# Three edits to a hybrid trunk layer on one core: margins for GpSimd, finer parts of the output projection, and another order of the front's loads and splits

## The chip, the cores and the metric

The kernel runs on 1 core of one Trainium2 chip. The metric is the device time of one execution in microseconds (us), lower is better; a kernel's time is the median of its runs. Engines: PE is TensorE (matmul), PEld its weight loads, DVE is VectorE, ACT ScalarE, POOL GpSimd, SP SyncE, which here issues nearly all DMAs.

## The reference

One decoder layer on x of 256 positions by 2048 features, float32. A norm, one input projection for all mixers, three mixers, an output projection with residual, a second norm and a gated MLP with a causal convolution, and a final norm:

```python
def reference(x, ...):
    h = rmsnorm(x, norm1_w)
    x = x + token_mixer(h, w_in, ..., w_out)
    h = rmsnorm(x, norm2_w)
    x = x + conv_ffn(h, ffn_w_up, ffn_conv_w, ffn_conv_b, ffn_w_down)
    return rmsnorm(x, final_norm_w)

def token_mixer(h, w_in, ...):
    proj = h @ w_in                      # D_IN = 6924 columns
    r_q, r_k, r_v, r_g, m_qk, m_v, m_o, m_gates, s_u = jnp.split(proj, splits, axis=-1)
    ret_out = silu(r_g) * head_groupnorm(retention(rotary(r_q), rotary(r_k), r_v), ret_gn_w)
    m_qk = silu(causal_dwconv(m_qk, mlstm_conv_w, mlstm_conv_b))
    i_pre, f_pre = jnp.split(m_gates + mlstm_gate_b, 2, axis=-1)
    mlstm_out = sigmoid(m_o) * head_groupnorm(mlstm(mq, mk, m_v, i_pre, f_pre), mlstm_gn_w)
    s5_out = s5(s_u, ...)                # diagonal complex state space model, gelu, gated by g @ glu_w
    return jnp.concatenate([ret_out, mlstm_out, s5_out], axis=-1) @ w_out
```

Retention and mLSTM have 6 heads of 128 features each, S5 has 512 features; together the 2048 rows of `w_out`. The MLP is 2048 to 2 x 5632 to 2048.

## The kernel before, in words

**Matmuls.** Every float32 weight chunk `wr` (up to 128 x 1024, from DRAM into one of four buffers) is split into a high part `wh` (a cast on ACT, `highs_to`) and a low part `wl` (a subtraction on DVE, `lows_to`); activations are split in the same way, the high part `d[:, :256]` by ACT, the low part `d[:, 256:]` by DVE. In the feature-major tiles (`fm_tile`, `fm_part`) the weights are stationary: for each K tile of 128 rows one matmul of 512 columns (high weights with both parts of x) and one of 256 (low weights with the high part of x). An output tile f is 128 features by 256 positions in one PSUM bank; 16 K tiles come as two chunks of 8. `chunk(i)` issues loads five items ahead, casts three and subtractions two ahead.

**Order.** Up to the end of the output projection the order of instructions on each engine is made by a planner in the kernel's own code: clocks `clk.pe`, `clk.dve`, `clk.act`, `clk.pool` are moved on by estimated costs (`run`), and everything beside the main chain of matmuls is a generator that yields what it waits for: `("dve", t)` until the DVE clock reaches t, `("pe", t)` until PE's does, `("obj", f)` until a condition holds. `pump()` runs between blocks of matmuls and steps the tasks that are due, first `hi_tasks` (evacuations of PSUM), then `lo_tasks` (heads, gates, S5) as long as the DVE clock is at most 0.35 us ahead of PE's. The clocks place instructions; on the chip the engines wait for each other by semaphores only. `after(t)` is such a wait for a result of POOL.

**Front.** x comes as 16 K tiles of 128 features. The first projection, `u` for S5, has four output tiles and is run K tile by K tile as the data arrive: `kts` holds four steps j of one K tile (weights 128 x 512) and then six of two (128 x 1024). Step j waits for its data, casts the weights, splits x by `n1` (from the parameters `pp0`), subtracts the weights, and issues 8 matmuls per K tile. `fill(n)` puts n of the 29 small DVE steps of the S5 exponentials (`s5_exps`, 128 x 16 each) in between; their 14th result starts POOL's chain `s5_params`. `square` collects x squared for the norm from step 4 on. SP issues x and weights in turn; ACT's queue issues `pp0`. Nine matmuls on ones (`warm`) precede the first real one. After the loop come six tiles for retention's q and k; between their blocks `first_norm` sums the squares on PE, POOL takes the power −1/2 (`rsqrt_`), and two transposes on PE (`norm_row`) make the row scale `rbc`.

**Heads.** `head_norm` normalises six heads (statistics on DVE, the power on POOL, scaling on ACT), multiplies by the gate, then for each head: two transposes on PE, the high part on ACT, the low part on DVE, into `mix[base + h]`. `mix[0..5]` is retention, `mix[6..11]` mLSTM, `mix[12..15]` S5 after `glu`. The gate of the second half of the mLSTM heads is the last tile (`tm_tile(7, ...)`) before the output projection.

**Output projection.** `parts` is its order: ((f, ...), k0, k1) takes K tiles k0 to k1 of tiles f; `None` stands for the S5 gate `glu`. PSUM has four `acc` banks and one `pair` of two. Tiles below `EARLY` = 4 are evacuated after K tile 12 (`early_evac`, which adds x) and get a second bank for K tiles 12 to 16. Tiles from `LATE` = 10 on are run whole after all parts. `out_evac` adds x or the early sum, splits by `n2` for the MLP and adds the square. Before a part the planner's loop `while any(k not in mix ...)` pumps until all its inputs are in the order.

After that the compiler's own scheduling takes over (MLP and final norm), which the change does not touch.

Of the kernel before, what the change touches and what calls it, by code (L numbers as in the profile page):

```python
# [40 lines left out]
def kernel(ctx: ExitStack, tc: tile.TileContext, a: dict, out: bass.AP):  # L41
# [54 lines left out]

    def after(t):

        return "dve", max(x[3] for x in wrote[t.tensor.name]) + 0.1

    def finish(gen):

# [223 lines left out]
    def add_stream(ap, n, step=CH):  # L326
        first = len(items)
        for c in range(0, n, step):
# [14 lines left out]
    st_tm.append(add_stream(a["wtm"][6], KT * 384, 768))  # L343


    EARLY, LATE = 4, 10

    parts = [((f,), 0, 8) for f in range(4)] + [((0, 1), 8, 12), ((2, 3), 8, 12)]
    parts += [((f,), 0, 8) for f in range(4, 8)] + [((4, 5), 8, 12), ((6, 7), 8, 12), ((8,), 0, 8), None,
                                                    ((9,), 0, 8), ((8, 9), 8, 12)]  # L350
    parts += [((f, f + 1), 12, 16) for f in (4, 6, 8, 0, 2)]
    wo_first = {}
    for part in parts:
        if part is None:
            st_glu = add_stream(a["glu"], 4 * 512)
        else:
            fs, k0, k1 = part
            wo_first[part] = len(items)
            items.append(([a["wout"][f][:, k0 * 128:k1 * 128] for f in fs], CH))
    st_out = [None] * LATE + [add_stream(a["wout"][f], KT * 128) for f in range(LATE, 16)]  # L360
    st_up = [add_stream(a["wup"][f], KT * 128) for f in range(2 * NFF)]
    st_dn = [add_stream(a["wdn"][f], NFF * 128) for f in range(14)]
    st_last = add_stream(a["wdt"], NFF * 256)
# [13 lines left out]
    def loads_to(i):  # L377
        while nxt[0] <= min(i, len(items) - 1):
            j = nxt[0]
            ap, n = items[j]  # L380
            if NS <= j < NU:

                t = s4()
            else:
                t = reuse("wr", wraw.tile([128, CH], F32, tag="wr", name=f"wr{j}"), 4)
            for i, z in enumerate(ap):
                nc.sync.dma_start(out=t[:, i * n // len(ap):(i + 1) * n // len(ap)], in_=z)
            if not auto[0]:
                free_at = max([x[3] for x in was_read.get(t.tensor.name, ())], default=0.0)
                clk.dma = max(clk.dma, free_at + 1.3) + n / 703.0  # L390
                landed(t, clk.dma + 0.91)
            if later:

                dst, src = later.pop(0)
                nc.sync.dma_start(out=dst, in_=src)
                clk.dma += free(dst) / 703.0
                landed(dst, clk.dma + 0.91)
                loaded.add(dst.tensor.name)
            raw[j] = t
            nxt[0] += 1  # L400
# [612 lines left out]
    def gates():  # L1013
# [19 lines left out]
            G.scalar_tensor_tensor(p, p, 1.0 / k, z2, op0=ADD, op1=MUL)  # L1033
        G.scalar_tensor_tensor(p, p, 1.0, z, op0=ADD, op1=MUL)
        G.scalar_tensor_tensor(lf, p, -2.0, lf, op0=MUL, op1=ADD)
        yield "dve", wrote[lf.tensor.name][-1][3]
        yield "pe", clk.dve + 0.2
        yield from grab("mis")
        ps = mis_t()
# [122 lines left out]
    manual = ctx.enter_context(ExitStack())  # L1162
    manual.enter_context(tc.manual_schedule())

    nc.scalar.dma_start(out=pp0, in_=a["pp"][:, :NP0])
    nc.gpsimd.memset(onesm, 1.0)

# [5 lines left out]
    warm = mis_t()  # L1173
    for _ in range(9):
        mm(warm[:, :128], lhsT=onesm, rhs=onesm, start=True, stop=True)
    clk.pe = 4.8

    xr, xat = [None] * 8, {}

# [15 lines left out]
    add(ret_heads())  # L1195
    add(gates())
    add(ml_heads())
    clk.dve = clk.pool = 3.3
    add(s5_params(s5_den()))
    add(s5_inputs())  # L1200
    for c in range(4):
# [10 lines left out]
    def first_norm():  # L1212
        r, ps = yield from norm_root(1)
        yield after(r)
        yield have(ident, rot)
        yield "pe", max(x[3] for x in wrote[r.tensor.name]) + 0.3
        bc = yield from norm_row(1, r, ps)
        rh = tn([128, 2])
        V.tensor_scalar(rh, r, 0.5, None, op0=MUL)
        for i in range(2):  # L1220
            V.tensor_tensor(rot[:, i * T:(i + 1) * T], rot[:, i * T:(i + 1) * T], bc, op=MUL)
        st.update(r=r, rh=rh, rbc=bc, cosr=rot[:, :T], sinr=rot[:, T:])
# [20 lines left out]
            next(exps, None)  # L1243

    for j, ks in enumerate(kts):
        fill(3 if j < 2 else 6)
        pump(until=max(last(raw[j].tensor.name), xat[ks[-1]]))
        if j > 1:
            highs_to(j)
        for k in ks:  # L1250
            d = s2(F32R)
            S.activation(d[:, :T], xr[k // 2][:, (k % 2) * T:(k % 2 + 1) * T], AF.Copy, scale=P("n1", k))
            xs.append(d)
        if j > 1:
            lows_to(j)
        for k in ks:
            V.scalar_tensor_tensor(xs[k][:, T:], xr[k // 2][:, (k % 2) * T:(k % 2 + 1) * T], P("n1", k),
                                   xs[k][:, :T], op0=MUL, op1=SUB)
        fill(4 if j < 2 else 0)
        lows_to(j)  # L1260
        loads_to(j + 4)
        if j + 4 == NU:
            rot = s2()
            raws = [s2() for _ in range(4)]
            later += [(ident, a["ident"]), (rot, a["rot"])]
            later += [(raws[i], a["s5b" if i < 2 else "s5c"][i % 2]) for i in range(4)]
            later += [(pp1, a["pp"][:, NP0:])]
            st["raws"] = raws
        if j >= NU - 6 and len(sqs) < 8:
            square()  # L1270
        hl = split.pop(j)
        for i, k in enumerate(ks):
            o = [slice(i * 512 + f * 128, i * 512 + (f + 1) * 128) for f in range(4)]
            for f in range(4):
                mm(ups[f], lhsT=hl[0][:, o[f]], rhs=xs[k], start=(k == 0), stop=False)
            for f in range(4):
                mm(ups[f][:, T:], lhsT=hl[1][:, o[f]], rhs=xs[k][:, :T], start=False, stop=(k == KT - 1))
# [105 lines left out]
    for part in parts:  # L1383
        if part is None:
            for f in range(EARLY, LATE, 2):
                get_x(f)
            glu()
            continue
        fs, k0, k1 = part
        if k0 == 8 and fs[0] < EARLY:  # L1390
            get_x(fs[0])
        while any(k not in mix for k in range(k0, k1)):
            clk.pe += 0.25
            pump()
        again = k0 == 12 and fs[0] < EARLY
        for f in fs:
            if f == 8 and k0 == 0:
                while len(bu) < 4:
                    clk.pe += 0.25
                    pump()  # L1400
                need("pair")
                room["pair"] -= 1
                pair = reuse("pair", ps_m.tile([128, 1024], F32, tag="pair", name=name("wo")), 1)
                wps[8], wps[9] = pair[:, :512], pair[:, 512:]
            elif f < 8 and (k0 == 0 or again):
                wps[f] = acc_t()
        hl = chunk(wo_first[part])
        for i, f in enumerate(fs):
            fm_part(wps[f], [z[:, i * CH // 2:] for z in hl], range(k0, k1), k0, mix,
                    12 if f < EARLY and not again else KT, first=12 if again else 0)  # L1410
        for f in fs:
            if f < EARLY and k1 == 12:
                add(early_evac(f, wps[f]), hi=True)
            elif k1 == KT:
                add(out_evac(f, wps[f], "acc" if f < 8 else "half"), hi=True)
        pump()
    get_x(LATE)
    for f in range(LATE, 16):
        if f + 2 < 16:
            get_x(f + 2)  # L1420
        add(out_evac(f, fm_tile(st_out[f], mix)), hi=True)
        pump()
    drain()
    xs2 = [xs2[f] for f in range(16)]
# [223 lines left out]
```

## Time and profile before

| | us |
|---|---|
| median of 3 runs (lowest, highest) | 1150.41 (1149.25, 1152.27) |
| time of the profiled execution | 1148.91 |
| its span, first to last instruction | 1147.1 |
| PE busy / DVE busy / ACT busy / POOL busy | 1131.2 / 879.0 / 628.0 / 76.5 |
| front: first real matmul to the end of `u` | 4.84 to 30.96 |
| output projection, first block | 299.45 |
| first tile that is run whole (f10) | 367.55 |

Rows of the timeline read: start us, duration us, engine, line, operation, out<-in, partitions x elements, count of merged instructions, and in brackets the idle time before it and who ended it. A line is often that of a helper (L235 every matmul, L183 every DVE operation, L218 every POOL operation), so rows are told apart by tiles and shapes: `wh`, `wl` are weights, `mis<-ident,s` a transpose of a head, `mis<-ident,t` a transpose of small rows such as the norm's. Rows of the waits read: engine and line that waited, for whom, total us, times, longest.

### The profile page before, as it was taken

The page shows a single profiled execution, that of the slowest core. Times are in us where ns is not written, and L with a number is a line of the kernel's source. Part 1 is how long each engine was busy: PE and PEld are TensorE (multiplying, and loading weights), DVE is VectorE, ACT ScalarE, POOL GpSimd, SP SyncE. Part 2 cuts the span into 40 slices and gives each one's busy share as a digit, 9 for nine tenths or more (in the row PEclk, how much of TensorE's full clock was granted, in tenths as well). Part 3 has the DMA queues.
Part 4 walks back from the last instruction along what each step waited for, and adds up shares of the span by engine and source line. Part 5 has one row for each costly group of instructions (what it writes and reads, how often), then busy time and mean ns, then how long its engine had stood idle before and what let it go on. Part 6 is the DMA issues. An engine that isn't in the chain of part 4 may idle for free.

```text
span 1147.1 us, 18124 instructions
## 1 busy us (share of the span) xinstructions
PE 1131.2 (99%) x6672; PEld 1010.3 (88%) x6672; DVE 879.0 (77%) x1527; ACT 628.0 (55%) x988; POOL 76.5 (7%) x171
## 2 busy tenths in 40 slices
PE   8999999999999999999999999999999999999997
PEld 7899889999888888888888888888888888888897
DVE  8899999999979777777777777777777655444454
ACT  7665565455647655555555555555555444444442
POOL 8407040010000000000000000000000000000000
PEclk9999999999999999999999999999999999999999
DMA  8657545556665655555555555555556566666662
GB/s 316 201 159 241 178 141 161 147 151 172 210 205 191 200 181 193 191 189 195 184 185 190 194 191 188 192 184 186 191 192 197 177 193 178 193 188 193 189 192 106
DMA packets 67625, 215.21 MB, mean 188 GB/s; under 512 B 7632, under 2 KB 9936, under 8 KB 67536
## 3 DMA queue, kind: packets, MB, share of 16 engines
q1 hardware_dynamic: 67392, 214.01, 58.8%
q8 instruction: 52, 0.85, 0.3%
q14 instruction: 37, 0.30, 0.1%
q10 hardware_dynamic: 144, 0.04, 0.0%
HBM read 211.92 MB, written 2.10 MB: 187 GB/s over the span
## 4 chain that ended last, share of the span: by engine, by line
PE 94%; POOL 3%; DVE 2%; issue 0%; DMA 0%; DVEq 0%; POOLq 0%
PE acc L235 90%; PE mis L235 3%; POOL t L218 2%; DVE s L183 2%; PE wo L235 1%; POOL tp L218 1%; DVE wl L183 1%; PE mis L239 0%; DMA pp<-in_pp_dram 0%; DVEq L1644 0%; PE pj L235 0%; DVE t L183 0%; DVEq L183 0%; POOLq L218 0%
## 5 line engine op out<-in xcount | busy, mean ns | idle before, releaser
L193 ACT CAST wh<-wr 128x1024 fp32r<-128x1024 f32 (+3 forms) x409 | 407.7, 998 | 417.2 <-PE acc L235 256.5
L235 PE MATMUL acc<-s,wh 128*128 128x512 f32 x2372 | 578.0, 392 | 6.0 <-DVE s L183 5.8
L183 DVE TENSOR_TENSOR wl<-wr,wh 128x1024 fp32r<-128x1024 f32 (+3 forms) x409 | 462.6, 1155 | 147.2 <-PE acc L235 96.1
L235 PEld LDWEIGHTS acc<-s,wh 128*128 128x128 f32 x2372 | 433.3, 188 | 90.0 <-DVE s L183 8.1
L235 PEld LDWEIGHTS acc<-s,wl 128*128 128x128 f32 x2372 | 309.8, 191 | 15.6 <-issue 0.7
L235 PE MATMUL acc<-s,wl 128*128 128x256 f32 x2372 | 317.1, 283 | 0.0
L183 DVE TENSOR_TENSOR s<-s,s 128x256 f32<-128x256 f32 (+5 forms) x264 | 124.7, 487 | 47.6 <-ACT s L202 41.5
L235 PE MATMUL acc<-wh,s 128*128 128x384 f32 (+2 forms) x632 | 158.0, 329 | 0.0
L183 DVE SCALAR_TENSOR_TENSOR s<-s,pp,s 128x255 f32<-128x255 f32 (+3 forms) x244 | 116.3, 479 | 6.1 <-ACT s L202 2.9
L235 PEld LDWEIGHTS acc<-wh,s 128*128 128x128 f32 x632 | 112.1, 189 | 2.0 <-ACT wh L193 1.1
L235 PE MATMUL acc<-wl,s 128*128 128x384 f32 (+2 forms) x316 | 103.0, 326 | 0.0
L183 DVE TENSOR_TENSOR s<-acc,s 128x256 f32<-128x256 f32 x142 | 59.2, 420 | 45.0 <-ACT s L193 41.7
L202 ACT ACTIVATE s<-s,pp 128x256 f32<-128x256 f32 (+1 forms) x146 | 82.2, 567 | 13.7 <-DVE s L183 12.6
L202 ACT ACTIVATE s<-s 128x256 f32<-128x256 f32 (+2 forms) x105 | 44.8, 428 | 34.6 <-DVE s L183 34.4
L218 POOL TENSOR_TENSOR t<-t,neg_half 128x2 f32<-128x2 f32 (+1 forms) x4 | 2.5, 633 | 882.3 <-DVE t L183 882.3
L235 PEld LDWEIGHTS acc<-wl,s 128*128 128x128 f32 x316 | 59.6, 189 | 0.1
L193 ACT COPY s<-acc 128x256 f32<-128x256 f32 x140 | 50.0, 360 | 11.1 <-PE acc L235 11.1
L235 PE MATMUL acc<-g,wh 128*128 128x512 f32 x196 | 49.5, 392 | 0.0
L183 DVE TENSOR_TENSOR s<-s,rbc 128x256 f32<-128x256 f32 x106 | 44.6, 424 | 5.6 <-ACT rbc L193 2.5
L235 PEld LDWEIGHTS acc<-g,wh 128*128 128x128 f32 x196 | 35.8, 188 | 6.9
L235 PEld LDWEIGHTS acc<-g,wl 128*128 128x128 f32 x196 | 25.4, 191 | 1.1
L235 PE MATMUL mis<-s,s 128*32 128x256 f32 (+6 forms) x216 | 25.8, 343 | 0.0
(107 smaller groups left out, 466.2 us busy)
## 6 DMA issues: line engine op xcount, KB each, us to landing
wr<-in_wup_dram SPq DMA_DIRECT2D x176, 512.0 KB, 4.5
wr<-in_wdn_dram SPq DMA_DIRECT2D x70, 512.0 KB, 4.2
wr<-in_wtm_dram SPq DMA_DIRECT2D x56, 384.0 KB, 3.3
wr<-in_wfm_dram SPq DMA_DIRECT2D x36, 512.0 KB, 4.1
wr<-in_wout_dram SPq DMA_DIRECT2D x22, 512.0 KB, 4.6
wr<-in_wdt_dram SPq DMA_DIRECT2D x11, 512.0 KB, 3.7
wr<-in_wout_dram SPq DMA_DIRECT2D x20, 256.0 KB, 3.8
s<-in_x_dram SPq DMA_DIRECT2D x14, 256.0 KB, 5.6
```

Source lines behind the costliest of these rows:

```text
L183: return real(o, *args, **kw)
L193: return nc.scalar.copy(o, i)
L202: return nc.scalar.activation(o, i, fn, **kw)
L218: return real(o, *args, **kw)
L235: nc.tensor.matmul(o, lhsT=lhsT, rhs=rhs, start=start, stop=stop)
```

## The change

1. Margins: `after` waits for POOL's result plus 1.0 us (0.1 before); the gates' transposes wait 3.0 us longer, the norm's transposes 1.8 (0.3 before).
2. Output projection: `EARLY` is 6 and `LATE` 12. Tiles 0 to 3 run K tiles 0 to 6 first, all four, then 6 to 12; tiles 4 to 11 in parts of 8 and 4 as before, with 10 and 11 in the `pair`. The last K tiles 12 to 16 run in pairs of tiles, and the whole tiles 12 to 15 (an integer in `parts`) stand between these pairs. x for tiles 12 and 14 is loaded just ahead of them.
3. Front: the first weight tile is issued on ACT's queue, ahead of `pp0`; each step splits x before it casts and subtracts the weights; the high part of K tile 0 is made on DVE; the small steps are spread, four per step in steps 0 to 3 and fewer per K tile later.

The planner's starting values (`clk.pe`, `clk.dve`, `clk.pool`) change with it.

```diff
     def after(t):
-        return "dve", max(x[3] for x in wrote[t.tensor.name]) + 0.1
+        return "dve", max(x[3] for x in wrote[t.tensor.name]) + 1.0
...
-    EARLY, LATE = 4, 10
-    parts = [((f,), 0, 8) for f in range(4)] + [((0, 1), 8, 12), ((2, 3), 8, 12)]
-    parts += [((f,), 0, 8) for f in range(4, 8)] + [((4, 5), 8, 12), ((6, 7), 8, 12), ((8,), 0, 8), None,
-                                                    ((9,), 0, 8), ((8, 9), 8, 12)]
-    parts += [((f, f + 1), 12, 16) for f in (4, 6, 8, 0, 2)]
+    EARLY, LATE = 6, 12
+    parts = [((f,), k, k + 6) for k in (0, 6) for f in range(4)]
+    parts += [((4,), 0, 8), ((5,), 0, 8), ((4, 5), 8, 12)] + [((f,), 0, 8) for f in range(6, 10)]
+    parts += [((6, 7), 8, 12), ((10,), 0, 8), None, ((8, 9), 8, 12), ((11,), 0, 8), ((10, 11), 8, 12)]
+    parts += [((6, 7), 12, 16), ((8, 9), 12, 16), 12, ((10, 11), 12, 16), ((0, 1), 12, 16), 13, ((2, 3), 12, 16), 14,
+              ((4, 5), 12, 16), 15]
...
+        elif isinstance(part, int):
+            st_out[part] = add_stream(a["wout"][part], KT * 128)
         else:
             fs, k0, k1 = part
             wo_first[part] = len(items)
-            items.append(([a["wout"][f][:, k0 * 128:k1 * 128] for f in fs], CH))
+            items.append(([a["wout"][f][:, k0 * 128:k1 * 128] for f in fs], len(fs) * (k1 - k0) * 128))
...
-                nc.sync.dma_start(out=t[:, i * n // len(ap):(i + 1) * n // len(ap)], in_=z)
+                (nc.sync if j else nc.scalar).dma_start(out=t[:, i * n // len(ap):(i + 1) * n // len(ap)], in_=z)
...
-        yield "dve", wrote[lf.tensor.name][-1][3]
+        yield "dve", wrote[lf.tensor.name][-1][3] + 3.0
...
+    loads_to(0)
     nc.scalar.dma_start(out=pp0, in_=a["pp"][:, :NP0])
...
-    clk.pe = 4.8
+    clk.pe = 4.5
...
-    clk.dve = clk.pool = 3.3
+    clk.dve = clk.pool = 3.7
...
-        yield "pe", max(x[3] for x in wrote[r.tensor.name]) + 0.3
+        yield "pe", max(x[3] for x in wrote[r.tensor.name]) + 1.8
...
     for j, ks in enumerate(kts):
-        fill(3 if j < 2 else 6)
         pump(until=max(last(raw[j].tensor.name), xat[ks[-1]]))
-        if j > 1:
-            highs_to(j)
         for k in ks:
-            d = s2(F32R)
-            S.activation(d[:, :T], xr[k // 2][:, (k % 2) * T:(k % 2 + 1) * T], AF.Copy, scale=P("n1", k))
+            d, x = s2(F32R), xr[k // 2][:, (k % 2) * T:(k % 2 + 1) * T]
+            if k == 0:
+                V.tensor_scalar(d[:, :T], x, P("n1", k), None, op0=MUL)
+            else:
+                S.activation(d[:, :T], x, AF.Copy, scale=P("n1", k))
             xs.append(d)
-        if j > 1:
-            lows_to(j)
+        fill(j == 0)
+        n = 2 if 0 < j < NS else 1
         for k in ks:
             V.scalar_tensor_tensor(xs[k][:, T:], xr[k // 2][:, (k % 2) * T:(k % 2 + 1) * T], P("n1", k),
                                    xs[k][:, :T], op0=MUL, op1=SUB)
-        fill(4 if j < 2 else 0)
+            fill(n)
         lows_to(j)
+        fill(n + (j == 0))
         loads_to(j + 4)
...
             square()
+            fill(1)
...
+        if isinstance(part, int):
+            if part % 2 == 0:
+                get_x(part)
+            add(out_evac(part, fm_tile(st_out[part], mix)), hi=True)
+            pump()
+            continue
...
-    get_x(LATE)
-    for f in range(LATE, 16):
-        if f + 2 < 16:
-            get_x(f + 2)
-        add(out_evac(f, fm_tile(st_out[f], mix)), hi=True)
```

More of the change, by code (lines that the diff above doesn't have):

```diff
@@ L343 @@
     st_tm.append(add_stream(a["wtm"][6], KT * 384, 768))
-    EARLY, LATE = 4, 10
-    parts = [((f,), 0, 8) for f in range(4)] + [((0, 1), 8, 12), ((2, 3), 8, 12)]
-    parts += [((f,), 0, 8) for f in range(4, 8)] + [((4, 5), 8, 12), ((6, 7), 8, 12), ((8,), 0, 8), None,
-                                                    ((9,), 0, 8), ((8, 9), 8, 12)]
-    parts += [((f, f + 1), 12, 16) for f in (4, 6, 8, 0, 2)]
-    wo_first = {}
+    EARLY, LATE = 6, 12
[4 more added lines that the diff above has]
+              ((4, 5), 12, 16), 15]
+    wo_first, st_out = {}, {}
     for part in parts:
@@ L358 @@
             wo_first[part] = len(items)
-            items.append(([a["wout"][f][:, k0 * 128:k1 * 128] for f in fs], CH))
-    st_out = [None] * LATE + [add_stream(a["wout"][f], KT * 128) for f in range(LATE, 16)]
+            items.append(([a["wout"][f][:, k0 * 128:k1 * 128] for f in fs], len(fs) * (k1 - k0) * 128))
     st_up = [add_stream(a["wup"][f], KT * 128) for f in range(2 * NFF)]
@@ L1388 @@
             continue
+        if isinstance(part, int):
[4 more added lines that the diff above has]
+            continue
         fs, k0, k1 = part
-        if k0 == 8 and fs[0] < EARLY:
+        if k1 == 12 and fs[0] < EARLY and fs[0] % 2 == 0:
             get_x(fs[0])
@@ L1396 @@
         for f in fs:
-            if f == 8 and k0 == 0:
+            if f == 10 and k0 == 0:
                 while len(bu) < 4:
@@ L1403 @@
                 pair = reuse("pair", ps_m.tile([128, 1024], F32, tag="pair", name=name("wo")), 1)
-                wps[8], wps[9] = pair[:, :512], pair[:, 512:]
-            elif f < 8 and (k0 == 0 or again):
+                wps[10], wps[11] = pair[:, :512], pair[:, 512:]
+            elif f < 10 and (k0 == 0 or again):
                 wps[f] = acc_t()
@@ L1408 @@
         for i, f in enumerate(fs):
-            fm_part(wps[f], [z[:, i * CH // 2:] for z in hl], range(k0, k1), k0, mix,
+            fm_part(wps[f], [z[:, i * (k1 - k0) * 128:] for z in hl], range(k0, k1), k0, mix,
                     12 if f < EARLY and not again else KT, first=12 if again else 0)
@@ L1414 @@
             elif k1 == KT:
-                add(out_evac(f, wps[f], "acc" if f < 8 else "half"), hi=True)
-        pump()
-    get_x(LATE)
-    for f in range(LATE, 16):
-        if f + 2 < 16:
-            get_x(f + 2)
-        add(out_evac(f, fm_tile(st_out[f], mix)), hi=True)
+                add(out_evac(f, wps[f], "acc" if f < 10 else "half"), hi=True)
         pump()
```

## The prediction

> **What bounds the kernel now.** I read the page first, then the waits of TensorE, then the timeline of PE around each wait, then DVE, ACT, POOL and the issues beside it. All times are from one profiled execution, whose span is 1147.1 us and whose own time is 1148.91 us; the median of the runs is 1150.41, 1.5 us above it. I take differences from the trace and subtract them from the median.
>
> ```profile
> span 1147.1 us, 18124 instructions
> PE 1131.2 (99%) x6672; PEld 1010.3 (88%) x6672; DVE 879.0 (77%) x1527; ACT 628.0 (55%) x988; POOL 76.5 (7%) x171
> GB/s 316 201 159 241 178 141 161 147 151 172 210 205 191 200 181 193 191 189 195 184 185 190 194 191 188 192 184 186 191 192 197 177 193 178 193 188 193 189 192 106
> ```
>
> ```profile
> PE acc L235 <- DVE s L183: 5.8, 5, 1.8
> PE mis L239 <- POOL t L218: 1.3, 1, 1.3
> ```
>
> PE is the bound: it computes nearly throughout, and the change takes no matmul away. All that can be won are the places where PE stands still. Ends of matmuls are modelled, so I go from start to start. A block of eight K tiles (eight 512-wide and eight 256-wide matmuls) takes 362.75 − 359.94 = 2.81 us; an input tile K of the first projection (four of each) therefore 1.40.
>
> ```profile
> 4.84 0.99 PE L235 MATMUL acc<-s,wh 128*128 128x512 f32 x2
> 7.71 0.50 PE L235 MATMUL acc<-s,wl 128*128 128x256 f32 x2
> 9.91 0.73 PE L235 MATMUL acc<-s,wh 128*128 128x512 f32 x2 [1.47 <-DVE s L183]
> 11.96 0.72 PE L235 MATMUL acc<-s,wh 128*128 128x512 f32 x2 [0.39 <-DVE s L183]
> 14.02 0.74 PE L235 MATMUL acc<-s,wh 128*128 128x512 f32 x2 [0.40 <-DVE s L183]
> 15.05 0.40 PE L235 MATMUL acc<-s,wl 128*128 128x256 f32 x2
> 30.96 2.00 PE L235 MATMUL acc<-s,wh 128*128 128x512 f32 x8
> ...
> 35.87 2.00 PE L235 MATMUL acc<-s,wh 128*128 128x512 f32 x8
> 39.14 0.43 PE L239 MATMUL mis<-ident,t 128*128 128x128 f32 x2 [1.26 <-POOL t L218]
> ...
> 299.45 2.01 PE L235 MATMUL acc<-s,wh 128*128 128x512 f32 x8
> 308.07 0.38 PE L239 MATMUL mis<-ident,s 128*128 128x128 f32 x2
> 311.09 0.38 PE L239 MATMUL mis<-ident,s 128*128 128x128 f32 x2
> 311.23 1.36 PE L235 MATMUL acc<-s,wh 128*128 128x512 f32 x3
> 314.31 0.50 PE L235 MATMUL acc<-s,wh 128*128 128x512 f32 x1 [1.72 <-DVE s L183]
> ...
> 359.94 1.09 PE L235 MATMUL acc<-s,wh 128*128 128x512 f32 x4
> 362.75 1.09 PE L235 MATMUL acc<-s,wh 128*128 128x512 f32 x4
> 365.08 0.63 PE L235 MATMUL acc<-s,wl 128*128 128x256 f32 x4
> 367.55 2.09 PE L235 MATMUL acc<-s,wh 128*128 128x512 f32 x8 [1.83 <-DVE s L183]
> ```
>
> Four stalls stand there. Front: the first four K tiles take 14.02 − 4.84 = 9.2 us and are worth 5.6, so 3.6 us are lost; from 14.02 to 30.96 (12 tiles, 16.8) nothing is. Norm: eight wide matmuls from 35.87 end their issue at 37.7 (0.23 each), the transposes start at 39.14: 1.4 us, for GpSimd's power. Mix: three matmuls from 311.23 take 0.7, the fourth starts at 314.31: 2.4 us, for the split of the last mLSTM head. Banks: four narrow matmuls from 365.08 take 0.5, f10 starts at 367.55: 2.0 us, because the evacuation on DVE that frees its PSUM bank is late. Together 9.4 us, the ceiling of the gain.
>
> **The change part by part. Front.** DVE is what the front waits for: a window row further down shows it busy 28.36 us of the 31.25 from 7.10 on.
>
> ```profile
> 3.25 0.17 DVE L183 TENSOR_SCALAR t<-pp 128x16 f32<-128x16 f32 x1 [3.25 <-DMA pp<-in_pp_dram]
> 3.83 0.48 DVE L183 SCALAR_TENSOR_TENSOR s<-s,pp,s 128x256 fp32r<-128x256 f32 x1
> 8.75 0.71 DVE L183 TENSOR_TENSOR wl<-wr,wh 128x512 fp32r<-128x512 f32 x1
> 10.08 0.81 DVE L183 SCALAR_TENSOR_TENSOR t<-t,t 128x16 f32<-128x16 f32 x4
> 13.49 0.87 DVE L183 SCALAR_TENSOR_TENSOR s<-s,pp,s 128x256 fp32r<-128x256 f32 x2
> ```
>
> ```profile
> 0.72 0.41 ACTq L1165 DMA_DIRECT2D pp<-in_pp_dram  x1
> 1.16 0.42 SPq L387 DMA_DIRECT2D wr<-in_wu_dram  x1
> 3.93 0.62 ACT L193 CAST wh<-wr 128x512 fp32r<-128x512 f32 x1 [0.17 <-DMA wr<-in_wu_dram]
> 10.86 1.05 ACT L193 CAST wh<-s 128x1024 fp32r<-128x1024 f32 x1 [1.00 <-DMA s<-in_wu_dram]
> ```
>
> The 29 small steps of the S5 exponentials (0.20 each by the row at 10.08) now all lie ahead of the first pair's x split, which ends at 13.49 + 0.87 = 14.36 with its first half at 13.97. After the change 18 of them lie ahead of that pair's low weights (four in each of the tiles 0 to 3, two between the pair's splits): 11 fewer, −2.2 us. Three things are added. The high part of x for K tile 0 moves from ACT to DVE: no row has a 128x256 tensor-scalar, the bounds are 0.17 (16 columns) and 0.48 (split of 256), I take 0.33. The second half of the pair's x split now precedes its weights: 0.40. And the parameters (pp) are issued second on ACT's queue: 0.44 later by the issue rows at the least, so 3.69 for 3.25; at the most behind 256 KB of weights and the 128 KB of x1, 3.93 plus 0.41 (128 KB at 316 GB/s) = 4.35. I take 3.9, near the time at which that weight tile lands now: +0.65. So DVE has the pair's low weights at 13.97 − 2.2 + 0.33 + 0.40 + 0.65 = 13.15, and PE, which needs them at 15.05 now, runs them 1.9 us earlier. The cast at 10.86 ends at 11.9, ahead of that, so transfers don't set it. Afterwards a pair costs DVE two splits, a weight subtraction, an add of squares and four small steps, close to PE's 2.81, for the 11 steps left; I take 0.2 off. Front: −1.7 us, between −0.7 (late parameters, DVE behind for some pairs) and −2.5. PE can't start before its warm-up ends at 4.8 in any case, so a first split at 3.9 + 0.33 + 0.2 + 0.48 = 4.9 costs 0.1 there, counted in the bounds.
>
> The Trainium skill, page "DMA: Bandwidth & Descriptors", section "Queues, rings and completion order", says that a DMA engine takes one issuer's ring in order and goes round among the rings packet by packet. By that the parameters can't overtake the weight tile in front of them and x1 shares the engines with both: they would land at the late bound, and the sum would be 0.45 us smaller. No run shown here has a weight tile in ACT's ring.
>
> On SP, every load after the first weight tile is issued one slot (0.44 to 0.47) earlier; the queue has no other work. ACT's second issue ends before its table load matters, and its first cast waits for data at 3.93 anyway: nothing.
>
> **Margins.** The norm's transposes move by a whole block, since tasks enter PE's order only between blocks: the planner, whose clock sets the order alone, puts the power some 1.1 us after the sums; with 0.3 on top that is within the next block of 2.81, with 1.8 it is past it. So PE reaches them one block later in its order.
>
> ```profile
> 7.13 0.60 POOL L218 TENSOR_TENSOR t<-pp,t 128x16 f32<-128x16 f32 x1
> 38.35 0.73 POOL L218 TENSOR_TENSOR t<-t,neg_half 128x2 f32<-128x2 f32 x1
> ```
>
> ```profile
> 7.10:38.35 31.25, 28.48 (x159) 23.74 (x157) 28.36 (x55) 23.35 (x40) 27.86 (x58) 1.00 0.85 319
> ```
>
> (Length, then busy us and count of PE, PEld, DVE, ACT and POOL; clock, DMA share, GB/s.) POOL runs 58 instructions in 31.25 us ahead of the power, 0.54 each. Its chain starts when the 14th small step is done; that now comes in tile 3, about 9.7 instead of 7.1. PE reaches the transposes at 37.7 − 1.7 + 2.8 = 38.8. The planner issues the S5 steps by its clock, so a chain that starts 2.6 later and is cut off 1.7 earlier has 4.3 / 0.54 = 8 fewer, 50, ahead of the power: 9.7 + 50 × 0.54 + 0.73 = 37.4. It fits, −1.4 us; with all 58 it would end at 41.8 (a rival below). The row scale is a block later for the first evacuations, which have freed their banks by then. The margin of 1.0 on the head norms and of 3.0 on the gates defer work whose readers are far off:
>
> ```profile
> 117.48 0.44 PE mis L239 x4
> ...
> 189.35 1.22 PE mis L235 x6
> ```
>
> The gates' transposes at 117 are first read by the mLSTM scores at 189: nothing, unless a plan shifted by other parts loses that cover, when the margin itself (1 to 3 us) is the price.
>
> **Output projection, mLSTM heads.** The first four blocks needed mix 0 to 7, then 8 to 11 at 311.2, 11.8 us after 299.45. Now four parts of six K tiles (2.1 us each, 8.4 in all) need retention alone, and the next needs mix 11 at 8.4 + 0.3 + five wide matmuls (1.15) = 9.85 us: about 2.5 earlier than now. What moves with it: the transposes enter between parts, so every 2.1 instead of every 3.02 us (308.07 to 311.09). The first head's came at 5.6 us and now comes after the third part (6.3), the second's after the fourth (8.4), the third's right behind, in the waiting loop. From there an ACT and a DVE step of some 0.5 us each per head give mix 11 at about 10.4 if DVE is free and 11.6 with one weight subtraction (1.2) in front. The wait is 0.5 to 1.8, I take 1.2 for 2.4: −1.2 us, with bounds +2.8 (the chain doesn't move, the need does) and −2.4.
>
> **Output projection, tail.** Five pairs in a row (K tiles 12 to 15) cost DVE 364.48 − 360.54 = 3.94 us each and PE 2.81.
>
> ```profile
> 360.54 1.22 DVE L183 TENSOR_TENSOR wl<-wr,wh 128x1024 fp32r<-128x1024 f32 x1
> 364.48 1.22 DVE L183 TENSOR_TENSOR wl<-wr,wh 128x1024 fp32r<-128x1024 f32 x1
> ...
> 326.00:340.00 14.00, 14.00 (x93) 11.74 (x92) 8.62 (x11) 5.69 (x7) 0.00 (x0) 1.00 0.73 237
> ```
>
> DVE falls behind by 1.13 a pair, 5.6 us over five, and 2.0 of it shows. Now a whole tile (PE 5.6; DVE two subtractions of 1.22 and one evacuation of (3.94 − 1.22) / 2 = 1.36, so 3.8) stands after the second, fourth, fifth and sixth pair and gives 1.8 back each time: the lag goes 1.1, 2.3, 0.5, 1.6, 2.7, 0.9, 2.0, 0.2, 1.4, 0 and never passes 2.7, less than the 3.6 that were hidden before. Every bank is written again two parts or more after its last reader. The cost: two more tiles are evacuated twice (two DVE steps of 0.42 and an ACT copy each, 1.7 us on DVE), ahead of the gate stage, where DVE now idles 14.00 − 8.62 = 5.4 us. If that cover is gone, the 1.7 us add to the lag, which then reaches 4.4 and shows 0.8. Loads of x for f12 and f14 move on SP past the weight loads before them, but stand a whole tile (5.6) ahead of their reader. The gate stage itself comes two blocks (5.6) later in PE's order: more cover. −1.7 us, between +1 (the lag shows at the FFN) and −2.0.
>
> The sum: 1.7 + 1.4 + 1.2 + 1.7 = 6.0; 1148.9 − 6.0 = 1142.9 for such an execution, 1150.4 − 6.0 = 1144.4 for the median.
>
> **The rivals.** Everything closes: 9.0 of the 9.4 us, 1141.4. For it: PE has other work at each place; against: DVE is nearly full.
> The output projection only moves its waits (need 2.5 earlier at the heads, lag at the FFN) and front and norm alone pay: −3.1, 1147.3. For it: DVE, not the order, is late at 314.31 and 367.55.
> GpSimd is late again: all 58 instructions ahead of the power, 41.8 against 38.8, a stall of 3.0 for 1.4: −3.0 in all, 1147.4. The Trainium skill, page "GPSIMD Engine Reference", section "Key points", says that GpSimd contends with VectorE instructions that have two SBUF inputs; the chain now runs beside them for longer.
> Slower, the other side: the three heads still advance one DVE round of 3.02 us at a time, and the first transposes come only after the fourth part: mix 11 at 8.4 + 3 × 3.02 = 17.5 against 9.85, a stall of 7.6 for 2.4. The rest gains 4.8, the balance is +0.4: 1150.8, and 1152 if the tail closes only half. It decides from a stall of 7.2 on; for it speaks the spacing of the heads' rows now, against it the waiting loop, which issues them at once.
> The front doesn't do what it says (parameters at 4.35, DVE behind in each pair): 0.7 instead of 1.7, 1145.4, inside the range.
>
> **How the numbers follow.** Forecast (with the weak front) 0.52; all closes 0.15; output projection moves only 0.15; GpSimd late 0.08; heads slower 0.10. A change of 0.3% (3.45 us) is about what a measurement of this kernel can tell from none. Forecast and ceiling lie beyond it but for a tail of 0.03, of the next two (3.1 and 3.0 won, with a spread of 1) a third does; of the heads' rival two thirds lie beyond it on the other side; so faster 0.71, same 0.22, slower 0.07. The range runs from the ceiling, 1141.0, to 1149.5, above the two small gains and short of the heads' rival; the forecast's own is 1142.4 to 1146.4.
>
> **What would show it.** The front: narrow matmuls of the first pair near 13.2 and the first block after the projection near 29.2 for 30.96. Norm: no idle PE before the two transposes, and POOL's power before them. Mix: one idle PE stretch of about 1.2 us 8 to 12 us into the output projection. Tail: none among the pairs, none at the FFN's first tile. The prediction is wrong if DVE's backlog only surfaces at another wait, or if the new plan opens a stall in the long stretch from 40 to 299 us, which has none of this size now.

## The result and the profile after

The changed kernel takes 1143.66 us (median of 4 runs, 1143.47 to 1144.18) against 1150.51 (4 runs, 1149.25 to 1152.27): ratio 0.9942, 95% interval 0.9929 to 0.9954. Predicted were 1144.4 us and faster. Its profiled execution took 1143.50 us for 1148.91 before, 5.41 less, while the medians differ by 6.85; where the other 1.4 come from is worked out under the sum, below. Two variants below had one execution far above the others (1229.85 us without the head norms' margin, the one that was profiled, and 2267.1 us without the norm's margin but with the pause); the ratios leave these out, and the medians move by 0.1 us with them.

The page of the changed kernel, span and busy times:

```profile
span 1141.6 us, 18166 instructions
PE 1130.1 (99%) x6672; PEld 1009.8 (88%) x6672; DVE 878.4 (77%) x1534; ACT 628.3 (55%) x991; POOL 76.2 (7%) x171
```

The matmuls are the same; what went is idle time of PE, and the waits of PE show which:

```profile
PE mis L239 <- DVE s L183: 2.5, 2, 2.1
PE acc L235 <- DVE s L183: 1.2, 2, 0.9
PE acc L235 <- DVE t L183: 1.1, 1, 1.1
```

PE's waits for DVE in the main matmuls (L235) fell from 5.8 us in five to 2.3 in three, and the wait of 1.3 for POOL is gone. The 2.1 us at L239 stand at the very end in both kernels. The timeline of PE after the change, at the places that the prediction named:

```profile
5.85 0.70 PE L235 MATMUL acc<-s,wh 128*128 128x512 f32 x2 [1.14 <-DVE t L183]
12.28 0.73 PE L235 MATMUL acc<-s,wh 128*128 128x512 f32 x2 [0.32 <-DVE s L183]
13.55 0.50 PE L235 MATMUL acc<-s,wl 128*128 128x256 f32 x2
29.56 2.00 PE L235 MATMUL acc<-s,wh 128*128 128x512 f32 x8
39.82 2.00 PE L235 MATMUL acc<-s,wh 128*128 128x512 f32 x8
41.66 0.38 PE L239 MATMUL mis<-ident,t 128*128 128x128 f32 x2
...
250.45 0.34 PE L235 MATMUL acc<-wh,s 128*128 128x384 f32 x1
251.22 0.44 PE L239 MATMUL mis<-ident,s 128*128 128x128 f32 x2 [0.44 <-DVE s L183]
...
297.74 1.55 PE L235 MATMUL acc<-s,wh 128*128 128x512 f32 x6
306.57 0.38 PE L239 MATMUL mis<-ident,s 128*128 128x128 f32 x2
306.70 1.39 PE L235 MATMUL acc<-s,wh 128*128 128x512 f32 x5
308.99 0.50 PE L235 MATMUL acc<-s,wh 128*128 128x512 f32 x1 [0.89 <-DVE s L183]
...
366.17 2.00 PE L235 MATMUL acc<-s,wh 128*128 128x512 f32 x8
368.01 1.07 PE L235 MATMUL wo<-s,wh 128*128 128x512 f32 x4
```

The first matmul starts at 5.85 (4.84 before), and still the projection ends earlier, at 29.56 for 30.96. At 41.66 the norm's transposes start without idle time. At 251.22 stands a wait that the kernel before did not have. At 308.99 the mix wait is left with 308.99 − 306.70 − 5 × 0.23 = 1.1 us of the 2.4, and among the tail's pairs nothing waits (eight matmuls from 366.17 end their issue at 368.0, where the next start).

### The profile page after: what moved, and what is told of

Its sections match the earlier page's. It is cut to its first block, busy times and chain, and to the rows that moved or that the text cites. A ratio compares the mean times of both kernels' runs of the same rounds, so it can differ in the third digit from the quotient of the medians.

```text
span 1141.6 us, 18166 instructions
## 1 busy us (share of the span) xinstructions
PE 1130.1 (99%) x6672; PEld 1009.8 (88%) x6672; DVE 878.4 (77%) x1534; ACT 628.3 (55%) x991; POOL 76.2 (7%) x171
## 4 chain that ended last, share of the span: by engine, by line
PE 72%; DVE 1%; DVEq 0%; issue 0%
PE acc L235 70%; PE wo L235 1%; PE mis L235 1%; DVE s L183 0%; PE mis L239 0%; DVEq L1652 0%; DVE t L183 0%
## 5 line engine op out<-in xcount | busy, mean ns | idle before, releaser
L235 PE MATMUL acc<-s,wh 128*128 128x512 f32 x2372 | 578.6, 392 | 2.4 <-DVE s L183 1.2
L235 PEld LDWEIGHTS acc<-s,wh 128*128 128x128 f32 x2372 | 432.6, 188 | 84.9 <-DVE s L183 1.3
L235 PEld LDWEIGHTS acc<-s,wl 128*128 128x128 f32 x2372 | 310.1, 191 | 15.5 <-DVE wl L183 0.5
L235 PE MATMUL acc<-s,wl 128*128 128x256 f32 x2372 | 317.0, 283 | 0.1
L183 DVE TENSOR_TENSOR s<-s,s 128x256 f32<-128x256 f32 (+4 forms) x266 | 125.5, 487 | 45.6 <-ACT s L202 41.7
L235 PE MATMUL acc<-wh,s 128*128 128x384 f32 (+2 forms) x632 | 158.4, 329 | 0.0
L235 PEld LDWEIGHTS acc<-wh,s 128*128 128x128 f32 x632 | 112.2, 189 | 2.3 <-issue 1.0
L235 PE MATMUL acc<-wl,s 128*128 128x384 f32 (+2 forms) x316 | 103.0, 326 | 0.0
L235 PEld LDWEIGHTS acc<-wl,s 128*128 128x128 f32 x316 | 59.6, 189 | 0.0
L235 PE MATMUL acc<-g,wh 128*128 128x512 f32 x196 | 49.5, 392 | 0.0
L235 PEld LDWEIGHTS acc<-g,wh 128*128 128x128 f32 x196 | 35.8, 188 | 6.9
L235 PEld LDWEIGHTS acc<-g,wl 128*128 128x128 f32 x196 | 25.4, 191 | 1.1
L235 PE MATMUL mis<-s,s 128*32 128x256 f32 (+6 forms) x216 | 26.1, 343 | 0.0
```

Of the source, the lines that this page charges most:

```text
L183: return real(o, *args, **kw)
L235: nc.tensor.matmul(o, lhsT=lhsT, rhs=rhs, start=start, stop=stop)
```

## The experiments

All are timed beside the kernel before; a ratio below 1 is faster. The parts alone come first.

**The front alone** (`loads_to(0)` first, the new loop over `kts`; margins and output projection as before).

> The kernel before with the front's edits alone (first weight tile on ACT's queue ahead of the parameters, x split ahead of its weights, small steps spread, the planner's starting clocks). Theory, that the parts add: the first projection ends near 29.6 us instead of 30.96 as in the changed kernel, so -1.4 us there; the norm's transposes keep their margin of 0.3 and are reached 1.4 us earlier while GpSimd's chain starts 3 us later, so their stall grows from 1.4 to some 2.5 us: total -0.5 us. Rival, that the front's gain is kept whole: -1.4 us. Rival, that GpSimd's late chain (58 instructions ahead of the power) is paid in full: stall 3 us or more, total 0 to +1 us.

Measured: 1155.64 us, ratio 1.0044 (1.0029 to 1.0059): slower by 4.8. The timeline of PE and, behind it, the windows (length, busy us of PE, PEld, DVE, ACT, POOL; clock, DMA share, GB/s):

```profile
112.48 0.27 PE L239 MATMUL mis<-ident,t 128*6 128x128 f32 x1
117.62 0.49 PE L239 MATMUL mis<-ident,t 128*6 128x128 f32 x3 [4.87 <-POOL t L218]
```

```profile
112.00:117.50 5.50, 0.75 (x4) 0.27 (x2) 5.50 (x10) 0.00 (x0) 5.02 (x6) 1.00 0.81 256
117.50:121.00 3.50, 3.38 (x11) 2.67 (x12) 1.74 (x5) 2.28 (x4) 0.31 (x2) 0.59 0.84 284
```

The gates' transposes wait 5.0 us for GpSimd, and behind the wait the granted clock is 0.59 for 3.5 us. The norm keeps a wait of 0.95, the bank wait its 2.0.

**The output projection alone.**

> The kernel before with the output projection's edits alone (EARLY 6, LATE 12, parts of six K tiles, whole tiles between the pairs). Theory: everything up to the output projection is unchanged, the wait for the last mLSTM head falls from 2.4 to about 1.1 us and the bank wait of 2.0 is gone: -3.3 us. Rival: the waits sit where they do because DVE is full, the part alone only moves them: -1 us or less, with idle PE at another tile or at the MLP's first tile.

Measured: 1145.91 us, 0.9959 (0.9944 to 0.9974): faster by 4.9. No bank wait; at the mix two waits, 1.06 and 0.77, for 2.4. All four executions have a mean granted clock of 0.998 (the share of the full TensorE clock that the profile shows as granted). At that clock the kernel before takes 1148.98 to 1149.56 us (under the sum, below), so about 3.3 of the 4.9 us are waits, as the theory had it; the rest, so read, is clock.

**The margins alone.**

> The kernel before with the three margins alone (1.0 for results of GpSimd, 3.0 for the gates, 1.8 for the norm's transposes). Theory: the norm's stall of 1.4 us goes, and the 1.4 us that the changed kernel loses between 200 and 299 us (a retention head's transpose waits 0.6 us at 250) come from the margin of 1.0 on the head norms, so they show here too: total 0 to -0.5 us. Rival: those losses come from the front's shift of GpSimd's chain, not from the margins: -1.4 us here and no stall near 250.

Measured: 1151.58 us, 1.0009 (0.9999 to 1.0018): nothing. The norm's wait is gone, but DVE waits 3.33 us for GpSimd in the gates, and PE has new waits of 0.85, 1.07 and 1.22 us ahead of 124.13, 128.94 and 343.57. No wait stands near 250. GpSimd's first step of the gates takes 7.52 us here, for 0.89 in the kernel before; the next runs show what that means.

Alone the parts give +4.8, −4.9 and +0.7, which is +0.6; together they give −6.85. The next two runs show most of the reason.

**The front with the gates' margin.**

```diff
-        yield "dve", wrote[lf.tensor.name][-1][3]
+        yield "dve", wrote[lf.tensor.name][-1][3] + 3.0
```

> The front's edits as in the front alone, and the one margin of 3.0 on the gates beside it; the norm's and the head norms' margins and the output projection stay as before. Theory: the front alone was slow because the gates' transposes came too early in TensorE's order for GpSimd's later chain (a wait of 5.0 us at 112.5 and half a granted clock for 3.4 us after it, some 1.7 us). With the margin that wait is gone: 1155.6 - 5.0 - 1.7 = 1149, within 1.5 of it, no wait over 1 us near 112, and the norm's wait of about 1 us at 38.7 still there. Rival: the front's shifted plan is late in general, the wait reappears at another reader and the time stays above 1153. Second rival: the front pays in full once the gates are covered (1.4 us won at 30): 1148.5 or less.

Measured: 1155.24 us, 1.0034 (1.0020 to 1.0048). My theory fell: the margin was not what was missing. The transposes no longer wait, but POOL and DVE show the cause one step earlier:

```profile
85.78 11.27 POOL L218 TENSOR_SCALAR t<-t 128x12 f32<-128x12 f32 x1 [39.28 <-DVE t L183]
```

```profile
96.18 0.76 DVE L183 TENSOR_TENSOR s<-s,s 128x256 f32<-128x256 f32 x2
96.85 1.28 DVE L183 TENSOR_TENSOR s<-mis,s 128x512 f32<-128x512 f32 x2
...
106.66 0.23 DVE L183 RECIPROCAL t<-t 128x12 f32<-128x12 f32 x1 [5.96 <-POOL t L218]
```

GpSimd's first step of the gates, 12 columns, takes 11.27 us (in the profiled execution, 1157.82 us, the slowest of five). All that time DVE runs steps with two inputs in SBUF, each starting before the one ahead of it has ended (96.18 + 0.76 is past 96.85). It ends at 97.05, just after DVE has gone over to steps with an input in PSUM (`s<-mis,s`). I call this the lockout of GpSimd. The chain is so late that DVE, where the reciprocal stands in its order, waits 5.96 us, and PE waits for the low weights queued behind that, 2.1 us in two waits. Larger waits of this trace stand at the mix (1.63 and 1.35 us, half a clock from some 317 to 324); what makes those is not shown. The same first step in four other kernels (the kernel before; the front alone; the changed kernel; the front with a pause, below):

```profile
87.24 0.89 POOL L218 TENSOR_SCALAR t<-t 128x12 f32<-128x12 f32 x1 [45.19 <-DVE t L183]
```

```profile
85.65 7.52 POOL L218 TENSOR_SCALAR t<-t 128x12 f32<-128x12 f32 x1 [39.25 <-DVE t L183]
```

```profile
84.56 1.56 POOL L218 TENSOR_SCALAR t<-t 128x12 f32<-128x12 f32 x1 [38.88 <-DVE t L183]
```

```profile
85.70 0.89 POOL L218 TENSOR_SCALAR t<-t 128x12 f32<-128x12 f32 x1 [39.25 <-DVE t L183]
```

In the changed kernel it ends at 86.12, where DVE happens to wait for ACT; the row of DVE:

```profile
86.18 0.96 DVE L183 TENSOR_TENSOR wl<-wr,wh 128x768 fp32r<-128x768 f32 x1 [0.17 <-ACT wh L193]
```

**The front with a pause of DVE.** One more step, which computes nothing that is used:

```diff
         G.tensor_scalar(lf, f, 0.0, None, op0=ALU.min)
+        V.tensor_scalar(tn(sh), lf, 1.0, None, op0=MUL)
```

> The front alone, with one small step added on DVE: it copies the result of GpSimd's first step of the gates (128x12) and so makes DVE pause until that step is done. In the front alone that step took 7.52 us, from 85.65 to 93.17, while DVE ran two-input steps without a gap; before the change it took 0.89. Theory: DVE's gapless two-input steps lock GpSimd out. With the pause the step ends within 0.4 us after DVE's weight subtraction before it (near 86.7), the reciprocal at 104 and the gates' transposes at 112 no longer wait, and the time falls from 1155.6 by 5.0 and by 1.7 for the half clock behind it: 1149, within 1.5. Rival: the step is long by itself (7.5 us beside anything), then DVE pauses for it, and the time is 1160 or more. Second rival: the chain's later steps are starved in turn, the transposes still wait 2 us or more: 1152 to 1155.

Measured: 1148.04 us, 0.9974 (0.9964 to 0.9983). A step of 0.17 us on DVE takes 7.6 us off the front alone. The first step is back at 0.89 (last of the four rows above), and the timelines of DVE and PE show the pause and transposes that wait for nothing:

```profile
85.54 0.95 DVE L183 TENSOR_TENSOR wl<-wr,wh 128x768 fp32r<-128x768 f32 x1
86.63 0.17 DVE L183 TENSOR_SCALAR t<-t 128x12 f32<-128x12 f32 x1
...
116.14 2.00 PE L235 MATMUL acc<-s,wh 128*128 128x512 f32 x8
117.98 0.60 PE L239 MATMUL mis<-ident,t 128*6 128x128 f32 x4
```

So the front gains, if GpSimd is let in: 3.0 us by the ratio, but only some 1.5 at the same clock (six executions at 0.998 or 0.999, 1147.25 to 1148.10, for 1148.98 to 1149.56). In the changed kernel it is let in at one wait of DVE of 0.17 us, which none of the three edits was made for.

**The changed kernel without the norm's margin** (`+ 0.3` for `+ 1.8`).

> The changed kernel with the norm's margin back at 0.3; all else as changed. Theory: the norm's transposes come a block earlier in TensorE's order, ahead of GpSimd's power, and wait for it 1.0 to 1.5 us at about 37.5: 1143.7 + 1.2 = 1144.9 (1144.6 to 1145.4). Rival: by the front's new order the sums themselves stand a block later in the plan, the power is ready by then, and the margin does nothing: 1143.7, no wait.

Measured: 1147.19 us, 0.9958 (0.9942 to 0.9975), 3.5 above the changed kernel, where I expected 1.2. The timeline of PE:

```profile
39.90 0.43 PE L239 MATMUL mis<-ident,t 128*128 128x128 f32 x2 [0.79 <-POOL t L218]
...
122.89 0.92 PE L235 MATMUL mis<-s,s 64*128 64x256 f32 x6 [0.69 <-ACT s L193]
127.71 1.38 PE L235 MATMUL mis<-s,s 64*128 64x256 f32 x8 [0.91 <-DVE s L183]
```

From start to start these three are 0.95, 0.85 and 1.07 us, and the mix wait is 1.71 for 1.06. GpSimd's first step of the gates takes 7.52 us here too.

**The same with the pause of DVE.**

> The changed kernel with the norm's margin back at 0.3 (1147.2, with the same 7.52 us step of GpSimd in the gates) and the same small pause of DVE. Theory: the waits of 0.85 us at 122 and of 1.07 at 126.4 come from the late gates and go, as does part of the 1.7 at 311; the norm's own 0.95 at 38.8 stays: 1147.2 - 1.9 = 1145.3, down to 1144.6. Rival: these waits come from the norm's earlier place in the order, nothing changes: 1147.2 within 0.4.

Measured: 1144.29 us, 0.9939 (0.9922 to 0.9955): 2.9 less by the one small step. The norm's wait stays (39.76 in the timeline of PE), the other two are gone:

```profile
39.76 0.43 PE L239 MATMUL mis<-ident,t 128*128 128x128 f32 x2 [0.80 <-POOL t L218]
...
121.26 0.92 PE L235 MATMUL mis<-s,s 64*128 64x256 f32 x8
```

So of the 3.5 us the norm's margin itself is worth 0.6 to 0.95; the rest was the lockout, which came back with the shifted plan.

**The old tail in the changed kernel.**

```diff
-    parts += [((6, 7), 12, 16), ((8, 9), 12, 16), 12, ((10, 11), 12, 16), ((0, 1), 12, 16), 13, ((2, 3), 12, 16), 14,
-              ((4, 5), 12, 16), 15]
+    parts += [((6, 7), 12, 16), ((8, 9), 12, 16), ((10, 11), 12, 16), ((0, 1), 12, 16), ((2, 3), 12, 16),
+              ((4, 5), 12, 16), 12, 13, 14, 15]
```

> The changed kernel with its last part in the old manner: the six pairs of K tiles 12 to 15 in a row, then the four whole tiles. Theory: DVE falls behind by 1.1 us in each pair, 6.8 in all, and a wait of 2 to 3 us for a bank shows at the last pair or the first whole tile, with the chance of half a granted clock for 3.4 us behind it: 1143.7 + 2 to 4.5 = 1145.7 to 1148.2. Rival: the pairs alone are not what made DVE late (the loads or the evacuations of the tiles before were), no wait of over 0.5 us shows, 1143.7 to 1144.2.

Measured: 1147.71 us, 0.9961 (0.9946 to 0.9976), 4.05 above the changed kernel. PE's timeline and the windows:

```profile
370.94 0.64 PE L235 MATMUL acc<-s,wl 128*128 128x256 f32 x4
373.40 2.01 PE L235 MATMUL acc<-s,wh 128*128 128x512 f32 x4 [1.83 <-DVE s L183]
```

```profile
370.00:373.40 3.40, 1.57 (x10) 1.19 (x8) 3.40 (x9) 2.99 (x7) 0.00 (x0) 1.00 0.61 218
373.40:376.90 3.50, 3.50 (x10) 2.95 (x11) 3.50 (x9) 2.85 (x7) 0.00 (x0) 0.51 0.34 117
376.90:380.00 3.10, 3.10 (x18) 2.65 (x17) 3.10 (x8) 2.16 (x8) 0.00 (x0) 1.00 0.40 141
```

The bank wait is back, 2.0 us, and right after it the clock is 0.51 for 3.5 us, which costs 1.7: 3.7 in all. (This trace, 4.38 us above the changed kernel's, is 0.66 behind before the tail: the mix wait ends at 309.65 for 308.99.) The whole tiles between the pairs are what removes both.

**The parameters first.** In the changed kernel ACT's queue issues `pp0` ahead of `loads_to(0)` again (start clocks `clk.pe` 4.8, `clk.dve` 3.3).

> The changed kernel with the parameters issued ahead of the first weight tile on ACT's queue, and the planner's starting clocks set for it. Theory: the parameters landed at 4.7 because they stood behind the weight tile in ACT's ring; now they land near 3.3, the first matmul starts at 4.9 instead of 5.85 and DVE runs 1.4 us ahead, so the first projection ends at 28.2 to 28.6 instead of 29.56: about -1 us. Rival, that the sixteen transfer engines bound the front: the weight tile comes later by as much, the first matmul starts near 5.3 and the end moves by 0.3 us or less.

Measured: 1143.09 us (1143.05 to 1143.18), 0.9934 (0.9919 to 0.9949): 0.57 less than the changed kernel. DVE and PE:

```profile
3.53 0.17 DVE L183 TENSOR_SCALAR t<-pp 128x4 f32<-128x4 f32 x1 [3.53 <-DMA pp<-in_pp_dram]
...
5.46 0.97 PE L235 MATMUL acc<-s,wh 128*128 128x512 f32 x2 [0.27 <-ACT wh L193]
```

The parameters are there 1.23 us earlier, PE starts 0.39 earlier, since now the weight tile's cast is what it waits for (it begins at 4.78 for 4.19). The first projection ends at 29.27, 0.29 earlier: the rival's case, not the theory's 1 us.

**That, without the head norms' margin** (`after` at `+ 0.1`).

> The changed kernel with the small parameters issued ahead of the weight tile on ACT's queue (1143.1), and the margin on the head norms back at 0.1. Theory: the margin of 1.0 puts seven scaling steps of ACT in a row and is what makes TensorE wait 0.60 us at 250.2 and 0.27 at 263.7, and without it these two waits go: 1143.1 - 0.9 = 1142.2. Rival: the waits come from the plan as a whole (the output projection's or the front's edits shift it), they stay or move, and the time is 1143.1 within 0.3. Other side: without the margin the head norms' transposes wait for their roots, several times 0.5 us: 1144 or more.

Measured: 1143.03 us, 0.9922 (0.9906 to 0.9939). Nothing, so the margin neither costs nor brings anything here. My theory for the wait at 251 fell: the next run has the small margin too, and a wait of 0.61 ahead of 251.18.

**The second round of the first four output tiles, cut anew.**

```diff
-    parts = [((f,), k, k + 6) for k in (0, 6) for f in range(4)]
+    parts = [((f,), 0, 6) for f in range(4)] + [((0, 1, 2, 3), 6, 8), ((0, 1), 8, 12), ((2, 3), 8, 12)]
```

> The kernel with the parameters first and the head norms' margin back (1143.0), with the output projection's second round of four parts (six K tiles each) cut anew: first K tiles 6 and 7 of all four output tiles (retention alone, 2.8 us), then K tiles 8 to 11 of two at a time. The last mLSTM head is then needed at 8.4 + 2.8 + 0.3 + 0.7 = 12.2 us into the projection, not at 9.85. Theory: the wait of 1.06 us near 307 goes: 1142.0 (1141.7 to 1142.3). Rival: the part's load has four pieces with rows of 1 KB and comes late, or the four banks that are freed together hold up the next tile: a wait of 0.5 to 1.5 takes its place, 1142.5 to 1143.5.

Measured: 1143.96 us, 0.9935 (0.9918 to 0.9951): 0.9 worse than without it. The timeline of PE:

```profile
309.31 0.38 PE L239 MATMUL mis<-ident,s 128*128 128x128 f32 x2
309.45 0.95 PE L235 MATMUL acc<-s,wh 128*128 128x512 f32 x3
312.07 0.50 PE L235 MATMUL acc<-s,wh 128*128 128x512 f32 x1 [1.68 <-DVE s L183]
```

The need moved 2.3 us later as meant, but the last head's transposes moved too, from 306.57 in the changed kernel to 309.31, with the projection's start at 297.74 and 297.70: tasks enter only between parts, and the new part is 2.8 us long. Neither of my two reasons for a failure (loads, banks) was it: three matmuls of the part had run, and the fourth, which reads the last head, waited for DVE.

**The parameters first, with the pause of DVE.**

> The changed kernel with the parameters ahead of the weight tile (1143.1) and the small pause of DVE for GpSimd's first step of the gates. Theory: with the pause that step takes 0.9 us where it took 1.56, the gates are 1 to 2 us earlier, and the waits of 0.60 at 250 and 0.27 at 264, which the run with the pause and the norm's margin at 0.3 did not have, go: 1142.3 (1142.0 to 1142.6), the wait of 1.06 at 307 stays. Rival: these waits belong to the place that the norm's margin gives the later work, the pause changes nothing there: 1143.1 within 0.3, with 0.60 still at 250. Other side: the pause costs DVE 0.4 us where it is full, 1143.5.

Measured: 1144.59 us, 0.9951 (0.9938 to 0.9963), 1.5 worse than without the pause. The waits at 250 and 264 are gone, as the theory had it, but PE's timeline has others, a head's transposes and two at the mix, and one in the gate stage:

```profile
305.38 0.44 PE L239 MATMUL mis<-ident,s 128*128 128x128 f32 x2 [0.42 <-DVE s L183]
307.27 0.51 PE L235 MATMUL acc<-s,wh 128*128 128x512 f32 x1 [0.51 <-DVE s L183]
308.87 0.50 PE L235 MATMUL acc<-s,wh 128*128 128x512 f32 x1 [1.09 <-DVE s L183]
...
344.50 0.50 PE L235 MATMUL mis<-s,wh 128*128 128x512 f32 x1 [1.06 <-DVE s L183]
```

Which step of the plan makes these is not settled either. The first step already ran in 1.56 us, so the pause had little to win (it takes 0.89 here); that it only gave the later work other places is my reading, not shown. The best kernels here are those with the parameters first, 1143.03 and 1143.09.

## Why the prediction held, and where it did not

**Front: 1.7 predicted, 1.40 measured** (30.96 − 29.56). The step that was mis-sized is the landing of the parameters: bounds of 3.69 and 4.35, 3.9 taken, 4.76 measured. The rows after the change, issues on ACT's queue and the first readers:

```profile
0.71 0.41 ACTq L390 DMA_DIRECT2D wr<-in_wu_dram  x1
1.15 0.46 ACTq L1170 DMA_DIRECT2D pp<-in_pp_dram  x1
4.19 0.62 ACT L193 CAST wh<-wr 128x512 fp32r<-128x512 f32 x1 [1.05 <-DMA wr<-in_wu_dram]
4.76 0.17 DVE L183 TENSOR_SCALAR t<-pp 128x4 f32<-128x4 f32 x1 [4.76 <-DMA pp<-in_pp_dram]
```

The parameters come 0.57 us after the weight tile in front of them. The Trainium skill, page "DMA: Bandwidth & Descriptors", section "Queues, rings and completion order", has each DMA engine take an issuer's ring in order, without a promise that transfers complete in that order. The rows agree, and so do the other traces: parameters read first at 4.61 to 4.84 and the tile at 4.00 to 4.23 in the seven with the tile issued first, 3.29 to 3.53 and 4.65 to 5.05 in three with the parameters first. The low weights of the first pair ran at 13.55 for the 13.15 predicted, and the recovery afterwards came as reckoned.

**Norm: 1.4 predicted; right in the effect, wrong in its numbers.** GpSimd's chain started at 10.55 (9.7 predicted), ran 52 steps (50) of 0.54 us and had the power at 39.75 (37.4):

```profile
39.02 0.73 POOL L218 TENSOR_TENSOR t<-t,neg_half 128x2 f32<-128x2 f32 x1
```

That would have been late for the arrival I had, 38.8; but the transposes came at 41.66, since the sums, too, had moved by a block. By the same main matmuls in both traces PE's lead is 3.1 to 3.2 us past the norm and still at 244 us; I take 3.17.

**From 40 to 299: 0 predicted, 1.46 lost.** The lead is 299.45 − 297.74 = 1.71 at the output projection, so the loss lies behind 244 us. The only wait of size is that at 251 (0.60), then 0.27 at 264; the rest is small. The prediction named this as what would make it wrong and gave it no price. The head margin does not cause it. The wait at 251 stands in the changed kernel and three of its variants (parameters first, old tail, second round cut anew: 0.60 to 0.61, each with 1.56 us for the first gates step), and in no part alone, nor with the pause, nor without the norm's margin; which order of steps makes it stays open.

**Mix: 1.2 predicted, about 1.2 measured** (1.1 left of 2.4), with the last head's transposes at 8.8 us after the start of the projection (306.57 − 297.74), 8.4 predicted.

**Tail: 1.7 predicted, 2.0 to 2.1 measured.** No wait is left, and the run with the old order shows the 2.0 back. Its second value is not in a trace of the kernel before and not in my sum: that wait is followed by half a clock in four of the six traces that have it (last section). The lead is 5.4 us at the end; the terms above make 1.40 + 1.77 − 1.46 + 1.2 + 2.05 = 5.0, the rest is in small pieces.

**The sum.** By traces 5.4 were won for 6.0 predicted; the medians differ by 6.85. The 45 runs of the kernel before in the experiments fall in steps: 1148.98 to 1149.56 us with a mean granted clock of 0.998 (7 runs; the profiled execution, 1148.91, has 0.998 too), 1150.32 to 1151.11 with 0.995 to 0.996 (17), 1151.54 (one), and 1152.04 to 1152.68 with 0.994 to 0.995 (20). Half a clock for 3.4 us costs 1.7 us, 0.0015 of the mean clock, so I read these as none, one and two such windows. Of the kernel before only an execution with none is traced. The margins alone and the front with a pause were traced with exactly one such window while TensorE works, each at a mean clock of 0.996, and 1.9 and 1.4 us above the median of their executions at 0.997 to 0.999. All runs of the changed kernel are at 0.998 or 0.999 (1143.47 to 1144.18). I subtracted trace differences from a median that, so read, holds one window: the missed 1.46 and the unforeseen 1.4 cancelled, which is luck.

**The rivals.** GpSimd late was right as a danger and had the wrong place: not the chain ahead of the norm (52 steps, in time) but a single step of the gates at 85 us. The heads' rival on the slow side did not come, as the transposes entered every 2.3 us. That the output projection only moves its waits is refuted by its run alone. Not everything closed: 1.1 us are left at the mix and 0.6 are new at 251. The weak front had its condition (parameters late, past even its 4.35), but not its price: 1.40 for 0.7.

## What to carry to other kernels

A small step on GpSimd can last almost as long as VectorE's unbroken run of steps with two inputs in SBUF (11.27 us here for a step that otherwise took 0.89): look for the longest single step on GpSimd, not for its mean, and give it a gap by letting VectorE read its result. That took 7.6 and 2.9 us off two kernels here and added 1.5 to a third, where the step was short already. In a kernel whose order a planner writes, parts measured alone do not add up, because each shifts where such gaps fall; measure the parts, then look in every trace for the same few places. A wait of 2 us on the bounding engine can cost almost 4, so a median must be compared with a median and a trace with a trace.

## What the runs showed of the hardware

GpSimd's 128x12 step takes 0.89, 1.56, 7.52 or 11.27 us, and ends in each case 0.10 to 0.12 us after the end of a DVE step: at a pause of DVE, at a change to inputs in PSUM, and, in the kernel before (88.14) and the front alone (93.17), between two steps that follow without one. What decides whether it gets in there stays open: with the front's edits and the same order of steps on DVE it took 7.52 us in one trace and 11.27 in another. The Trainium skill, page "SBUF — State Buffer", section "Who interferes with whom", says that a DVE instruction with two SBUF inputs contends with a GpSimd instruction that reads SBUF and that the loser blocks until the other instruction has ended. The rows agree on who blocks and on the end; they go beyond it in that GpSimd lost to 24 instructions in a row (85.60 to 96.94), not to one.

Half a granted clock for 3.4 us followed waits of PE of 2.0 us (old tail, 0.51 from 373.4 to 376.9; front with a pause, 0.51 from 367.2 to 370.7; front alone, 0.51 from 374.0 to 377.5; margins alone, 0.56 from 371.3 to 374.8) and of 5.0 (front alone, from 117.5). It does not follow each of them: the profiled execution of the kernel before had the wait of 2.0 ahead of 367.55 and a clock of 1.00 after it, and so had the front with the gates' margin (ahead of 376.13). The Trainium skill, page "TensorE: Matmul & The Clock Gate", Part 1, gives the activity monitor of TensorE a free-running window of 3413 ns and two settings of the clock, full and half; the lengths and the 0.51 agree. A window that runs free would explain why the same wait is punished in one run and not in the next; no run here tested that.
